# A two-layer trunk on one core: the planner's durations of TensorE's products are set to other numbers

## The chip, the cores and the metric

The kernel runs on one core of a Trainium2 chip. The metric is the device time of one execution in microseconds (us), lower is better. Profile times count from the start of the profiled execution's span.

## The reference

A trunk of two layers works on 256 latent tokens and 256 context tokens of width 1024. In each layer the modulated input goes through one wide projection, then through three mixers side by side (a bidirectional gated linear attention, GLA, in chunks of 64; a latent attention, MLA, with low-rank queries and keys; a convolution module), and the merged result through an output projection. Then comes a gated FFN with a convolution of width 3. A LayerNorm closes both halves. In the last layer the context only feeds the latent stream.

```python
def _trunk_layer(x, xc, mod, cmod, p, cos, sin, last):
    shift1, scale1, gate1, shift2, scale2, gate2 = [m[:, None, :] for m in jnp.split(mod, 6, axis=-1)]
    ...
    y, yc = _token_mixer(x * (1 + scale1) + shift1, xc * (1 + cscale1) + cshift1, p, cos, sin, last)
    x = _layer_norm(DN_ALPHA * x + gate1 * y, p['ln1_g'], p['ln1_b'])
    x = _layer_norm(DN_ALPHA * x + gate2 * _conv_ffn(x * (1 + scale2) + shift2, p), p['ln2_g'], p['ln2_b'])
    ...

def _conv_ffn(h, p):
    u = _depthwise_conv(h @ p['ffn_wup'], p['ffn_dw'], p['ffn_db'])
    g, v = jnp.split(u, 2, axis=-1)
    return (jax.nn.silu(g) * v) @ p['ffn_wdown']
```

## The kernel before

All values are float32. A large product is made of three products of rounded parts (`mm3`): a weight tile comes raw by a DMA on SyncE's queue (`wr`, four buffers), ScalarE casts its rounded high part (`wh`, three buffers), VectorE subtracts it for the low part (`wl`, three buffers), and TensorE adds up wh·xh, wh·xl and wl·xh. The inputs (`xm`, and `gy`, `my`, `cy`, `hd` further on) are split in the same way. Such products are of type F32R and have 256 or 512 columns; the products of the GLA units, of the norms (`sq` and `macc` times a constant) and of the attention are plain F32.

VectorE also has work that isn't wanted soon: `jk`, the rows of the modulation (w_ada) for later norms, `cv`, the taps of the two convolutions, and `gt`, the gates of the merge. Between mixer and FFN stands a norm: VectorE forms the sums (`macc`), takes off the mean (`xa`), ScalarE squares (`sq`), VectorE adds up the squares; TensorE adds over partitions (`pm_1473` in layer 0), VectorE picks from it (`dg`, a reduction to `sm`), GpSimd takes the power (`sm_1484`), TensorE spreads it (`pm_1485`), VectorE scales `xa`, ScalarE modulates it to `xm` and casts.

No instruction is issued where the program's code calls it. Class `Order` stands in for the engines' interface: `add` records each instruction with its dependences, `cost` gives it a duration, and `plan` is a list scheduler that starts instructions on five in-order engines (`ENGS`) when inputs and buffers are free, the one with the least latest start first. `back` finds the latest starts from the end of a plan, and `best` goes through eight such rounds and keeps the order whose planned end is the smallest. `emit` (line 294) then issues everything in that order, so that every row of the trace has line L294, and rows are told apart by the names of their tiles. A tile's number is counted up by the program; a row of an order names it, a row of the trace doesn't.

The durations of `cost` thus decide the order in which each engine takes its instructions, for all engines, and nothing else.

## Time and profile before

| | |
|---|---|
| three runs | 1907.19, 1908.35, 1911.92 us |
| median | 1908.35 us |
| span of the profiled execution | 1908.6 us |
| TensorE busy | 1854.9 us, 97% |
| VectorE busy | 1616.0 us, 85% |
| ScalarE busy | 1001.4 us, 52% |
| DMA | 312 MB, 164 GB/s on average |

Busy TensorE time in the profile is the union of matmuls that overlap; a row's own duration is therefore longer than the distance from its start to the next one's. Where a rate is read, it is the count of rows by the time of a stretch that is full. Names: PE is TensorE, PEld its weight loads, DVE VectorE, ACT ScalarE, POOL GpSimd, SP SyncE.

### The profile page before, as it was taken

The page shows a single profiled execution, that of the slowest core. Times are in us where ns is not written, and L with a number is a line of the kernel's source. Part 1 is how long each engine was busy: PE and PEld are TensorE (multiplying, and loading weights), DVE is VectorE, ACT ScalarE, POOL GpSimd, SP SyncE. Part 2 cuts the span into 40 slices and gives each one's busy share as a digit, 9 for nine tenths or more (in the row PEclk, how much of TensorE's full clock was granted, in tenths as well). Part 3 has the DMA queues.
Part 4 walks back from the last instruction along what each step waited for, and adds up shares of the span by engine and source line. Part 5 has one row for each costly group of instructions (what it writes and reads, how often), then busy time and mean ns, then how long its engine had stood idle before and what let it go on. Part 6 is the DMA issues. An engine that isn't in the chain of part 4 may idle for free.

```text
span 1908.6 us, 30907 instructions
## 1 busy us (share of the span) xinstructions
PE 1854.9 (97%) x11868; PEld 1661.8 (87%) x11868; DVE 1616.0 (85%) x2801; ACT 1001.4 (52%) x1564; POOL 21.1 (1%) x22
## 2 busy tenths in 40 slices
PE   6999999999999999989999999999899999989997
PEld 2889998887888888968888999999899889989997
DVE  2799999999899985899999766797978998878865
ACT  1863454246666264564443445864444675667643
POOL 0000000000000000000000000000000000000000
PEclk9999999999999999989999999999999999999999
DMA  7533247733223586566555667623265327846563
GB/s 269 178 113 104 89 138 236 250 112 120 84 90 114 160 257 201 171 205 210 186 188 176 194 178 213 190 67 105 63 189 172 99 95 245 263 155 210 181 181 93
DMA packets 116628, 312.18 MB, mean 164 GB/s; under 512 B 13376, under 2 KB 39232, under 8 KB 116480
## 3 DMA queue, kind: packets, MB, share of 16 engines
q1 hardware_dynamic: 116480, 310.21, 51.2%
q8 instruction: 93, 1.52, 0.3%
q14 instruction: 55, 0.45, 0.1%
HBM read 284.73 MB, written 25.43 MB: 163 GB/s over the span
## 4 chain that ended last, share of the span: by engine, by line
PE 53%; DVE 2%; ACT 1%; issue 0%; POOL 0%; ACTq 0%; DVEq 0%; POOLq 0%
PE pm L294 53%; DVE e L294 1%; ACT wh L294 0%; ACT xa L294 0%; DVE att L294 0%; DVE xa L294 0%; ACT xm L294 0%; DVE wl L294 0%; POOL sm L294 0%; DVE kd L294 0%; DVE sm L294 0%; DVE dg L294 0%; DVE cv L294 0%; DVE qe L294 0%; ACT kc L294 0%
## 5 line engine op out<-in xcount | busy, mean ns | idle before, releaser
L294 PE MATMUL pm<-xm,wh 128*128 128x256 f32 (+1 forms) x3536 | 872.6, 338 | 14.4 <-ACT xm L294 9.8
L294 ACT CAST wh<-wr 128x1024 fp32r<-128x1024 f32 (+2 forms) x394 | 401.8, 1021 | 599.7 <-PE pm L294 479.4
L294 PEld LDWEIGHTS pm<-xm,wh 128*128 128x128 f32 x3536 | 607.5, 191 | 84.1 <-ACT xm L294 11.2
L294 PE MATMUL pm<-xm,wl 128*128 128x256 f32 (+1 forms) x1768 | 591.3, 336 | 0.2 <-DVE wl L294 0.2
L294 DVE TENSOR_TENSOR wl<-wr,wh 128x1024 fp32r<-128x1024 f32 (+1 forms) x398 | 471.3, 1186 | 138.9 <-ACT wh L294 132.2
L294 PEld LDWEIGHTS pm<-xm,wl 128*128 128x128 f32 x1768 | 337.0, 191 | 37.7 <-issue 4.0
L294 DVE SCALAR_TENSOR_TENSOR cv<-h,vec,cv 128x512 f32<-128x512 f32 (+1 forms) x480 | 276.8, 611 | 1.1
L294 DVE SCALAR_TENSOR_TENSOR jk<-wr,crep 128x1024 f32<-128x1024 f32 x160 | 194.6, 1216 | 2.5 <-DMA wr<-in_w_adt_dram 2.4
L294 PE MATMUL pm<-hd,wh 128*128 128x256 f32 x1056 | 191.0, 283 | 0.0
L294 PEld LDWEIGHTS pm<-hd,wh 128*128 128x128 f32 x1056 | 165.0, 192 | 0.2
L294 PE MATMUL pm<-hd,wl 128*128 128x256 f32 x528 | 149.4, 283 | 0.0
L294 DVE SCALAR_TENSOR_TENSOR u<-pm,vec,u 128x255 f32<-128x255 f32 (+1 forms) x180 | 106.2, 601 | 1.8 <-ACT u L294 1.0
L294 PEld LDWEIGHTS pm<-hd,wl 128*128 128x128 f32 x528 | 101.3, 192 | 0.0
L294 PE MATMUL pm<-wh,xm 128*128 128x256 f32 x512 | 93.7, 283 | 0.0
L294 PEld LDWEIGHTS pm<-wh,xm 128*128 128x128 f32 x512 | 80.4, 192 | 0.4 <-issue 0.2
L294 PE MATMUL pm<-wl,xm 128*128 128x256 f32 x256 | 72.9, 285 | 0.0
L294 PE MATMUL pm<-ay,wh 128*128 128x256 f32 x384 | 69.7, 284 | 0.0
L294 ACT ACT_TABLE_LOAD x50 | 64.2, 1283 | 5.6 <-DMA ct<-in_cT_dram 2.4
L294 ACT ACTIVATE u<-pm,vec 128x256 f32<-128x256 f32 (+1 forms) x90 | 59.0, 660 | 12.9 <-PE pm L294 12.9
L294 PE MATMUL pm<-gy,wh 128*128 128x512 f32 (+1 forms) x256 | 62.5, 336 | 0.0
L294 PE MATMUL pm<-cy,wh 128*128 128x512 f32 (+1 forms) x256 | 62.5, 336 | 0.0
L294 PE MATMUL pm<-my,wh 128*128 128x512 f32 (+1 forms) x256 | 62.3, 336 | 0.0
(190 smaller groups left out, 2668.9 us busy)
## 6 DMA issues: line engine op xcount, KB each, us to landing
wr<-in_w_in_dram SPq DMA_DIRECT2D x124, 512.0 KB, 4.2
wr<-in_w_up_dram SPq DMA_DIRECT2D x90, 512.0 KB, 4.3
wr<-in_w_adt_dram SPq DMA_DIRECT2D x80, 512.0 KB, 3.7
wr<-in_w_sq_dram SPq DMA_DIRECT2D x72, 512.0 KB, 4.2
wr<-in_w_down_dram SPq DMA_DIRECT2D x48, 512.0 KB, 3.8
wr<-in_w_down_dram SPq DMA_DIRECT2D x24, 384.0 KB, 3.1
wr<-in_w_ada_dram SPq DMA_DIRECT2D x16, 512.0 KB, 4.4
wr<-in_w_v_dram SPq DMA_DIRECT2D x16, 512.0 KB, 3.8
```

What stands on the lines that cost most here:

```text
L294: method(*args, **kw)
```

## The change

In `Order.cost` the durations of two kinds of TensorE products change. One of F32R operands with n columns was n/2400 + 0.003 us, and is n/2400 + 0.0133 us (512 columns: 0.2163 to 0.2266; 256: 0.1097 to 0.1200). One of plain F32 was four times (n/2400 + 0.003), at least 0.42 us below 32 columns; it is 4n/2400 + 0.005, at least 0.222 (128 columns: 0.2253 to 0.2220; 1 column: 0.42 to 0.222). The set of instructions stays, but for the loads of ScalarE's function tables, which follow from the order: 52 where there were 50.

```diff
             if ins[0].dtype == F32R:
-                return n / 2400 + 0.003
+                return n / 2400 + 0.0133
             w = ins[0].shape[-1]
             if w <= 32:
                 return n / 2400 * 1.15 + 0.01
-            return max(4 * (n / 2400 + 0.003), 0.42 if n < 32 else 0.0)
+            return max(4 * n / 2400 + 0.005, 0.222)
```

What that does to the order is seen below, in three places; the rows stand in the order of the engine's list.

TensorE at the norm between mixer and FFN of layer 0, before: `pm_1506` and `pm_1514` are the first two tiles of the FFN's up-projection for one stream, `pm_1473` the norm's sum of squares for the other.

```order
L294 MATMUL pm_1506<-xm_1357,wh_1504 128x256
L294 MATMUL pm_1472<-macc_1471,cst 128x256
L294 MATMUL pm_1506<-xm_1357,wh_1504 128x256
L294 MATMUL pm_1514<-xm_1357,wh_1512 128x256 x2
L294 MATMUL pm_1473<-sq_1481,cst 128x256
L294 MATMUL pm_1506<-xm_1357,wl_1505 128x256
L294 MATMUL pm_1506<-xm_1358,wh_1504 128x256 x2
L294 MATMUL pm_1506<-xm_1358,wl_1505 128x256
```

The same place now, from the last product of `pm_1506` on:

```order
L294 MATMUL pm_1506<-xm_1364,wl_1505 128x256
L294 MATMUL pm_1514<-xm_1357,wl_1513 128x256
L294 MATMUL pm_1514<-xm_1358,wh_1512 128x256 x2
L294 MATMUL pm_1514<-xm_1358,wl_1513 128x256
L294 MATMUL pm_1514<-xm_1359,wh_1512 128x256 x2
L294 MATMUL pm_1514<-xm_1359,wl_1513 128x256
L294 MATMUL pm_1514<-xm_1360,wh_1512 128x256 x2
L294 MATMUL pm_1473<-sq_1481,cst 128x256
```

`pm_1473` stood behind 2 products of each tile; now the other 22 of `pm_1506` and 9 of `pm_1514` are ahead of it.

VectorE at the same place, before: `sq` are the sums of squares, `wl` the low parts of up-projection weights, `dg` and `sm` the norm's chain.

```order
L294 TENSOR_TENSOR xa_1463<-xa_1463,pm_1472 128x256
L294 TENSOR_TENSOR sq_1480<-sq_1479,sq_1480 128x256
L294 SCALAR_TENSOR_TENSOR jk_1466,mod_163<-wr_1464,crep 128x1024
L294 TENSOR_TENSOR sq_1481<-sq_1480,sq_1481 128x256
L294 TENSOR_TENSOR wl_1505<-wr_1503,wh_1504 128x1024
L294 TENSOR_TENSOR dg_1482<-pm_1473,cst 128x256
L294 SCALAR_TENSOR_TENSOR jk_1509,mod_163<-wr_1508,crep 128x1024
L294 TENSOR_REDUCE sm_1483<-dg_1482 128x2
L294 TENSOR_TENSOR xm_1364<-xm_1431,xm_1364 128x256
L294 TENSOR_SCALAR sm_1483<-sm_1483 128x2
L294 SCALAR_TENSOR_TENSOR jk_1510,mod_163<-wr_1508,crep 128x1024
L294 TENSOR_TENSOR wl_1513<-wr_1511,wh_1512 128x1024
```

And now:

```order
L294 TENSOR_TENSOR sq_1479<-sq_1478,sq_1479 128x256
L294 TENSOR_TENSOR wl_1521<-wr_1519,wh_1520 128x1024
L294 TENSOR_TENSOR sq_1480<-sq_1479,sq_1480 128x256
L294 SCALAR_TENSOR_TENSOR mod_163<-mod_163,vec_95 128x8
L294 TENSOR_TENSOR sq_1481<-sq_1480,sq_1481 128x256
L294 SCALAR_TENSOR_TENSOR jk_1509,mod_163<-wr_1508,crep 128x1024
L294 TENSOR_TENSOR dg_1482<-pm_1473,cst 128x256
L294 TENSOR_TENSOR wl_1526<-wr_1524,wh_1525 128x1024
L294 TENSOR_REDUCE sm_1483<-dg_1482 128x2
L294 SCALAR_TENSOR_TENSOR jk_1510,mod_163<-wr_1508,crep 128x1024
L294 TENSOR_SCALAR sm_1483<-sm_1483 128x2
L294 TENSOR_TENSOR wl_1535<-wr_1533,wh_1534 128x1024
```

`jk_1466` has gone ahead of the sums; `wl_1505` and `wl_1513` stand ahead of `sq_1478` and `sq_1479`, `wl_1521` between `sq_1479` and `sq_1480`; `wl_1526` and `wl_1535` have come into the chain behind `dg_1482`, and `jk_1517` follows on `wl_1535`.

VectorE in the first GLA unit of layer 1, before: `v` takes the values out of PSUM, `att` masks the scores, `e` and `kd` are decayed keys and queries.

```order
L294 TENSOR_TENSOR v_2216<-pm_2218,vb_2112 128x512
L294 TENSOR_TENSOR wl_2287<-wr_2285,wh_2286 128x1024
L294 COPY_PREDICATED att_2224<-lmask,pm_2227 128x512
L294 TENSOR_TENSOR wl_2291<-wr_2289,wh_2290 128x1024
L294 TENSOR_TENSOR e_2236<-cum_2219 128x128x2
L294 COPY_PREDICATED att_2224<-lmask,pm_2229 128x512
L294 TENSOR_TENSOR e_2236<-cum_2219 128x128x2 x2
L294 COPY_PREDICATED att_2224<-lmask,pm_2231 128x512
L294 TENSOR_TENSOR e_2236<-cum_2219 128x128x2
L294 TENSOR_TENSOR kd_2241<-kd_2241,pm_2240 128x512
L294 TENSOR_TENSOR kd_2245<-kd_2245,pm_2244 128x512 x2
L294 TENSOR_TENSOR e_2238<-cum_2219 128x256
```

And now:

```order
L294 TENSOR_TENSOR wl_2287<-wr_2285,wh_2286 128x1024
L294 TENSOR_TENSOR v_2216<-pm_2218,vb_2112 128x512
L294 TENSOR_TENSOR wl_2291<-wr_2289,wh_2290 128x1024
L294 COPY_PREDICATED att_2224<-lmask,pm_2227 128x512
L294 TENSOR_TENSOR e_2236<-cum_2219 128x128x2
L294 COPY_PREDICATED att_2224<-lmask,pm_2229 128x512
L294 TENSOR_TENSOR e_2236<-cum_2219 128x128x2 x2
L294 COPY_PREDICATED att_2224<-lmask,pm_2231 128x512
L294 TENSOR_TENSOR e_2236<-cum_2219 128x128x2
L294 COPY_PREDICATED att_2224<-lmask,pm_2233 128x512
L294 TENSOR_TENSOR e_2238<-cum_2219 128x256
L294 COPY_PREDICATED att_2224<-lmask,pm_2235 128x512
```

`wl_2287` and `v_2216` have changed places, and the copies of `pm_2233` and `pm_2235` have come ahead of the `kd` rows; the products e × kq and the four `kd` rows follow.

VectorE in the output projection of the GLA of layer 0, before (`wl_696` is row 409 of its list):

```order
L294 TENSOR_TENSOR wl_687<-wr_685,wh_686 128x1024
L294 SCALAR_TENSOR_TENSOR jk_674,mod_96<-wr_673,crep 128x1024
L294 SCALAR_TENSOR_TENSOR cv_285<-h_280,vec_94,cv_285 128x512
L294 SCALAR_TENSOR_TENSOR jk_675,mod_96<-wr_673,crep 128x1024
L294 SCALAR_TENSOR_TENSOR cv_274<-h_269,vec_94,cv_274 128x512
L294 TENSOR_TENSOR wl_696<-wr_694,wh_695 128x1024
```

And now (`wl_696` is row 420):

```order
L294 TENSOR_TENSOR wl_687<-wr_685,wh_686 128x1024
L294 SCALAR_TENSOR_TENSOR jk_675,mod_96<-wr_673,crep 128x1024
L294 TENSOR_TENSOR gt_648<-pm_658,gt_648 128x512
L294 SCALAR_TENSOR_TENSOR jk_683,mod_96<-wr_682,crep 128x1024
L294 TENSOR_TENSOR gt_660<-pm_667,gt_660 128x512
L294 SCALAR_TENSOR_TENSOR jk_684,mod_96<-wr_682,crep 128x1024
L294 TENSOR_TENSOR wl_696<-wr_694,wh_695 128x1024
```

Gates and modulation rows that stood behind `wl_696` are ahead of it; TensorE takes its tile at the same place as before.

## Rows read from the trace of the kernel before

**Rows 1.** The page: span, busy time of each engine with its share of the span and instructions, and from the costliest groups the loads of ScalarE's tables.

```profile
span 1908.6 us, 30907 instructions
PE 1854.9 (97%) x11868; PEld 1661.8 (87%) x11868; DVE 1616.0 (85%) x2801; ACT 1001.4 (52%) x1564; POOL 21.1 (1%) x22
...
L294 ACT ACT_TABLE_LOAD x50 | 64.2, 1283 | 5.6 <-DMA ct<-in_cT_dram 2.4
```

**Rows 2.** Busy time by stretch in two stretches of one kind of product each, 512 columns in the first and 256 in the second: the stretch and its length, then PE, PEld, DVE, ACT, POOL busy with counts, the granted clock of TensorE, the DMA engines' share and GB/s.

```profile
912.00:960.00 48.00, 48.00 (x213) 39.78 (x212) 46.75 (x70) 21.25 (x29) 0.00 (x0) 1.00 0.57 184
1824.00:1872.00 48.00, 48.00 (x403) 48.00 (x402) 27.84 (x37) 19.94 (x26) 0.00 (x0) 1.00 0.63 182
```

**Rows 3.** Busy time by stretch, with the columns of rows 2, for stretches in which TensorE isn't full and for 96 to 384 us.

```profile
0.00:48.00 48.00, 31.42 (x117) 11.91 (x117) 13.84 (x41) 7.05 (x12) 0.20 (x4) 0.93 0.79 269
...
96.00:336.00 240.00, 240.00 (x1451) 213.02 (x1450) 234.75 (x384) 117.15 (x145) 5.20 (x4) 1.00 0.43 138
336.00:384.00 48.00, 48.00 (x214) 39.74 (x213) 45.76 (x72) 10.48 (x11) 0.00 (x0) 1.00 0.78 248
...
792.00:840.00 48.00, 38.52 (x266) 35.54 (x265) 44.55 (x96) 33.16 (x69) 3.23 (x2) 0.89 0.53 174
...
1248.00:1296.00 48.00, 46.87 (x382) 45.89 (x382) 47.05 (x89) 27.84 (x41) 0.00 (x0) 1.00 0.20 65
...
1344.00:1392.00 48.00, 42.31 (x324) 40.88 (x323) 45.96 (x93) 18.27 (x28) 0.00 (x0) 0.96 0.15 45
...
1440.00:1488.00 48.00, 46.26 (x379) 45.47 (x378) 45.08 (x91) 23.11 (x37) 2.65 (x2) 1.00 0.60 187
...
1680.00:1728.00 48.00, 41.35 (x304) 39.42 (x304) 36.94 (x76) 32.67 (x65) 0.70 (x1) 0.93 0.51 166
...
1872.00:1908.00 36.00, 26.12 (x199) 25.01 (x197) 19.02 (x42) 12.15 (x23) 0.69 (x1) 0.90 0.22 69
```

**Rows 4.** Timelines at the norm between mixer and FFN of layer 0, engine by engine (VectorE, TensorE, GpSimd, ScalarE): start, duration, engine, line, operation, tiles, count, and in brackets the idle time before and what ended it.

```profile
813.25 0.75 DVE L294 TENSOR_TENSOR xa<-xa,pm 128x256 f32<-128x256 f32 x2
...
818.24 0.42 DVE L294 TENSOR_TENSOR sq<-sq,sq 128x256 f32<-128x256 f32 x1
818.58 1.22 DVE L294 SCALAR_TENSOR_TENSOR jk<-wr,crep 128x1024 f32<-128x1024 f32 x1
...
819.72 0.42 DVE L294 TENSOR_TENSOR sq<-sq,sq 128x256 f32<-128x256 f32 x1
820.06 1.22 DVE L294 TENSOR_TENSOR wl<-wr,wh 128x1024 fp32r<-128x1024 f32 x1
...
826.71 0.87 DVE L294 SCALAR_TENSOR_TENSOR xa<-xa,vec,pm 128x256 f32<-128x256 f32 x2 [0.68 <-PE pm L294]
...
820.20 1.22 PE L294 MATMUL pm<-sq,cst 128*128 128x256 f32 x2 [5.83 <-DVE sq L294]
...
822.14 0.41 PE L294 MATMUL pm<-xm,wl 128*128 128x256 f32 x1
...
824.06 0.41 PE L294 MATMUL pm<-xm,wl 128*128 128x256 f32 x1
...
829.99 0.50 PE L294 MATMUL pm<-xm,wh 128*128 128x256 f32 x2 [0.69 <-ACT xm L294]
831.25 0.50 PE L294 MATMUL pm<-xm,wh 128*128 128x512 f32 x1 [0.75 <-ACT wh L294]
...
823.93 1.51 POOL L294 TENSOR_TENSOR sm<-sm,mhalf 128x2 f32<-128x2 f32 x1 [22.23 <-DVE sm L294]
...
828.57 1.08 ACT L294 ACTIVATE xm<-xa,mod 128x256 f32<-128x256 f32 x2
```

**Rows 5.** Busy time by stretch around the same norm, with the columns of rows 2.

```profile
815.00:820.00 5.00, 0.00 (x0) 0.00 (x0) 5.00 (x14) 2.41 (x7) 0.00 (x0) 0.57 0.00 0
820.00:826.00 6.00, 5.80 (x24) 5.18 (x25) 5.82 (x11) 1.04 (x1) 1.51 (x1) 0.51 0.60 182
826.00:830.00 4.00, 3.31 (x29) 3.10 (x28) 3.32 (x6) 3.73 (x8) 0.00 (x0) 1.00 0.77 257
```

**Rows 6.** The first GLA unit of layer 1: timelines of VectorE and TensorE, and between them TensorE's waits in 1270 to 1284 us (who waited for whom, us in total, times, longest).

```profile
1270.62 0.69 DVE L294 TENSOR_TENSOR v<-pm,vb 128x512 f32<-128x512 f32 x1 [0.95 <-PE pm L294]
1271.23 1.22 DVE L294 TENSOR_TENSOR wl<-wr,wh 128x1024 fp32r<-128x1024 f32 x1
...
1282.08 0.71 DVE L294 COPY_PREDICATED att<-lmask,pm 128x512 f32<-128x512 uint8 x1
...
PE pm L294 <- DVE e L294: 1.1, 2, 0.9
...
1283.20 1.03 PE L294 MATMUL pm<-v,kd 128*128 128x256 f32 x4
```

**Rows 7.** TensorE's waits in the second GLA unit of layer 1, 1357 to 1383 us, with the same columns.

```profile
PE pm L294 <- DVE e L294: 5.1, 4, 3.2
```

**Rows 8.** Timelines of VectorE and TensorE at the norm of the MLA's keys in layer 1.

```profile
1480.34 1.22 DVE L294 TENSOR_TENSOR wl<-wr,wh 128x1024 fp32r<-128x1024 f32 x1
...
1484.60 1.16 PE L294 MATMUL pm<-cst,sm 128*128 128x128 f32 x8 [1.74 <-POOL sm L294]
```

**Rows 9.** Timelines of VectorE at `wl_696` and of TensorE at its first use.

```profile
356.42 1.23 DVE L294 TENSOR_TENSOR wl<-wr,wh 128x1024 fp32r<-128x1024 f32 x1
...
366.69 0.39 PE L294 MATMUL pm<-gy,wl 128*128 128x512 f32 x1
```

## Prediction

> **What bounds the kernel now.** I read the page's busy shares first, then the busy time by stretch, then the timelines around the stretches where TensorE is not full. TensorE is busy for 97% of the span, VectorE for 85%, ScalarE for 52% [rows 1]. In the stretch of 48 us that is nothing but 512-column products, 213 of them take 48.0 us, 0.225 us each; in one of 256-column products 403 take 48.0 us, 0.119 us each [rows 2]. The old numbers of the plan were 0.2163 and 0.1097, the new ones are 0.2266 and 0.1200: the new plan is told the truth, the old one was told a TensorE that is 4 to 8% too fast. But the instructions are the same, so wherever TensorE has been full it stays at the same rate, and the change can only move its idle time. The table by stretch shows how little of that there is [rows 3]: 16.6 us before 48 us, 9.5 in 792 to 840, 1.1 in 1248 to 1296, 5.7 in 1344 to 1392, 1.7 in 1440 to 1488, 6.7 in 1680 to 1728, 9.9 at the end. In the remaining stretches it is full, and there only a new wait could show. VectorE is nearly full beside it from 96 to 384 us (234.75 of 240, then 45.76 of 48).
>
> The order of the instructions is practically the same in the first 50 us and from 1680 us on, so the idle time there (33 us in the three places) stays: 0. That leaves four places.
>
> **1. The norm between mixer and FFN of layer 0, 810 to 834 us.** Before, VectorE sums the squares, ends the last sum (sq_1481) at 820.06 and only then makes wl_1505, the low part that the first FFN tile wants; TensorE waits 5.83 us, takes the sum's product pm_1473 at 820.20, and works at that tile while the norm's chain runs [rows 4]. Now VectorE makes wl_1505, wl_1513 and wl_1521 between the sums, and TensorE takes 31 products of the two tiles ahead of pm_1473.
>
> Start of the filling: from 813.25, where the sums' inputs begin, 12 short rows of VectorE (0.34 us from start to start, 818.24 to 818.58) give 817.3; wl_1505 follows and takes 1.14 (as a jk row of as many columns, 818.58 to 819.72). TensorE resumes at 818.4 and not at 820.2. The last sum: 817.3 + 3 × 1.14 + 4 × 0.34 + 0.1 = 822.2, so 2.1 later than before.
>
> Products ahead of pm_1473: the granted clock falls to half in this wait (0.57 in 815 to 820, 0.51 in 820 to 826, 1.00 from 826 on) [rows 5], and then nine products took 1.92 us (822.14 to 824.06), 0.213 each. Before, the half clock lasted 5.7 us after work was resumed; so 27 products at 0.213 and 4 at 0.119 take 6.2, and pm_1473 starts at 824.6 where it started at 820.2: +4.4. With a full clock it would be 822.1 (+1.9), with a half one throughout 825.0 (+4.8).
>
> From pm_1473 to GpSimd: before 3.73 us (820.20 to 823.93). Now: product 0.65 at a full clock, dg 0.34, wl_1526 1.14, the reduction 0.34, jk_1510 1.14, sm 0.3 = 3.9: GpSimd starts at 828.5. To xa: GpSimd 1.51 and the product pm_1485 with its hand-overs 0.74, so 830.75; wl_1535 and jk_1517 are put between sm and xa on VectorE, 2.3 us, and end at 830.7, hidden behind GpSimd. Before, xa started at 826.71: +4.1. From xa to the first product of the next tiles 3.28 us before (826.71 to 829.99), 3.2 now as no weight cast lies between on ScalarE: 834.0, +4.0.
>
> All the work in front of that product is the same set in both (both FFN tiles are complete), so the 4.0 is lost. Given back: before, 14 products, 2.1 us of work, took from 829.99 to 833.30, with 0.75 of waiting for wh_1534; now the casts and low parts are ready: -0.8 (0 to -1.2). And a second fall of the clock: the two tiles end at 824.6 + 0.5 + 15 × 0.119 = 827, then TensorE is idle for 7 us but for pm_1485, longer than the 5.83 us after which rows 5 show half clock. A half clock for 5.7 us costs 2.85 us of work where TensorE is the limit; right after the norm ScalarE is, with three rows like xm's 0.54 us (1.08 for two), 1.6, per feature tile against 1.4 of TensorE at full clock (six products of 0.119, three of 0.225), so I take half of it: +1.4 (0 to +2.85). Sum: 4.0 - 0.8 + 1.4 = **+4.6**. Bounds: with the clock full all the time 4.0 - 2.5 - 1.2 = +0.3; with all against it 4.0 + 0.4 + 2.85 = +7.2.
>
> [...]
>
> **2. The first GLA unit of layer 1, 1270 to 1283 us.** Before, TensorE waits twice, 1.1 us in all, for the products e × kq [rows 6], and VectorE had waited 0.95 for v's product. Now wl_2287 (1.14) is made in that wait, and one att copy (0.71) comes in: VectorE's chain behind v, which ran without a break from 1271.23 to 1282.08, where the last e × kq ended, has the same rows otherwise and is 1.14 - 0.71 = 0.4 shorter; it now ends on the last kd row at 1281.7, and the state products that started at 1283.20 can start at 1281.8. TensorE has 1.1 to give: I take **-1.3** (-1.1, the two waits, to -1.4, the whole shift).
>
> **3. The second GLA unit and the key norm of layer 1.** The second unit's four waits are 5.1 us, the longest 3.2 [rows 7]. Its chain on VectorE, from cum to the last e × kq, has the same rows in both orders and ends the wait, so the idle time stays; TensorE gets a little more done ahead of it, so it is not paid for behind: **+0.5** (-1.5 to +1.5, a row of 1.14 and one of 0.34 more or less on the chain). At 1484.60 TensorE waits 1.74 us for GpSimd; between dg and the reduction stands a low part of 1024 columns (1.14), now one of 384 columns (by its share 0.45) [rows 8]: -0.7; but low parts that the next tiles want come later there: **-0.5** (-0.7 to +2).
>
> **4. Layer 0's low parts, 96 to 385 us, where both engines are full.** Background rows of VectorE (jk, cv, gt) are moved ahead of the low parts of weights. The worst is wl_696: it ended at 357.6 and was first used at 366.69, 9.0 us of cover [rows 9]. It is now eleven rows further back in VectorE's list; at 0.71 (an att copy) to 1.14 us a row that is 8 to 12.5 us, so the cover may be short by up to 3.5. VectorE's own idle time in the stretch (2.24 of 48) takes up most of it, and what is done early is not done later. **+0.5** (0 to +3). Elsewhere in these stretches the covers stay positive. Two more table loads on ScalarE (52 where there were 50) are hidden by its 48% of idle time: 0, and 2.6 at 1.28 each [rows 1] if not.
>
> **Sum.** 4.6 - 1.3 + 0.5 - 0.5 + 0.5 = +3.8 on the profiled 1908.6 us, which stands 0.25 above the median of the three runs: 1912.4, so 1912 us, 0.2% slower. By the bounds alone: -3 to +12, or +15 with the table loads. What a measurement can tell from no change is about 0.3%, 5.7 us.
>
> **Rivals.**
> *It is faster.* The waits of the two GLA units of layer 1 go, since the plan now gives the plain F32 products there other times: 1.1 + 5.1, and 1.9 for the half clock behind the longest wait (a granted 0.96 over 1344 to 1392, so 0.04 × 48) [rows 3]. With the layer-0 norm at +0.3: 1908.6 - 8.1 + 0.3 = 1901. For it: in place 2 the order does just this. Against it: in the second unit the chain is as long as before. It decides from where the norm costs less than 2 us and the second unit gains 4. Chance 0.2.
> *It comes out even.* The norm's second cold spell doesn't come, pm_1473 isn't held up by the half clock, and the gain of the first unit pays for it: 0.3 - 1.3 + 0.5 = 1908. Inside the same bound as the forecast. Chance 0.15.
> *It is clearly slower.* The norm costs its upper bound, 7, by the two cold spells, and the low parts of layer 0 come late at several places at once (3), as VectorE is full beside TensorE from 96 us on: 1908.6 + 10 - 1.3 = 1917. For it: the clock in rows 5 and eleven rows at wl_696. Against: the idle time of VectorE. Chance 0.35.
>
> **How the numbers follow.** The forecast has 0.3, with the even case 0.45, faster 0.2, slower 0.35. The likeliest lies at 1912, with 1908 to 1914 for it alone; 8 in 10 reach from the faster rival's 1901 to beyond the slower one's 1917, its other unknowns (2 at the key norm, 2.6 of table loads) added: 1901 to 1921.
>
> **What the profile will show.** Right: a TensorE that resumes near 818 us, pm_1473 near 824, the first product after the norm near 834, a granted clock under 1 in 834 to 840; 0 instead of 1.1 us idle near 1280; the waits near 1370 to 1380 as before. Wrong if idle time of TensorE shows between 100 and 400 us in amounts above 3 us, if the longest wait near 1378 is gone, or if the norm costs nothing since the early products are taken at a full clock.

## The result and the profile after

The changed kernel takes 1930.53 us (median of four runs, 1927.73 to 1932.15), the kernel before 1909.21 us (four runs, 1907.19 to 1911.92). The ratio is 1.0106, with a 95% interval of 1.0093 to 1.0120: slower by 21 us. The forecast was 1912, its range ended at 1921.

The page of the changed kernel, in the lines of [rows 1]:

```profile
span 1930.4 us, 30899 instructions
PE 1866.2 (97%) x11868; PEld 1669.2 (86%) x11868; DVE 1613.6 (84%) x2801; ACT 1003.7 (52%) x1566; POOL 25.8 (1%) x22
...
L294 ACT ACT_TABLE_LOAD x52 | 66.7, 1283 | 5.7 <-DVE e L294 2.5
```

The same products, VectorE 2.4 us less busy, and one number that stands out: GpSimd is busy for 25.8 us, not 21.1, with the same 22 instructions. The busy time by stretch, with the columns of [rows 3], moved along where the work lies later:

```profile
0.00:48.00 48.00, 31.27 (x117) 11.95 (x117) 13.87 (x41) 7.08 (x12) 0.20 (x4) 0.92 0.78 270
96.00:336.00 240.00, 236.27 (x1426) 209.18 (x1425) 233.30 (x386) 113.81 (x143) 9.38 (x4) 0.99 0.39 127
336.00:384.00 48.00, 48.00 (x214) 39.75 (x213) 43.15 (x75) 10.08 (x10) 0.00 (x0) 1.00 0.85 278
804.00:852.00 48.00, 34.98 (x235) 32.74 (x234) 44.75 (x95) 30.44 (x64) 3.05 (x2) 0.82 0.54 180
1260.00:1308.00 48.00, 47.42 (x386) 46.53 (x385) 47.85 (x89) 34.07 (x47) 0.00 (x0) 1.00 0.21 67
1364.00:1412.00 48.00, 41.05 (x298) 39.53 (x297) 45.36 (x92) 17.58 (x25) 0.00 (x0) 0.89 0.09 28
```

Where TensorE never waited in 240 us [rows 3], it now waits 3.7 us, and its clock is below 1.00 there (0.99); GpSimd's four powers in that stretch take 9.38 us, not 5.20. Idle time above 3 us between 100 and 400 us was one of the prediction's own signs of being wrong.

To place the loss I gave each product the distance from start to start that its kind has at the full clock (F32R of 256 and 512 columns 0.120 and 0.227 us, plain F32 of 128 columns 0.223, two rows of the trace at 0.112, and so on), and took what the next one starts later than that as lost. The work so counted is 1812.9 us in both kernels; lost are 81.8 us before and 103.5 after, by places of the program (in brackets the prediction's numbers of its places):

| place | before | after | difference | predicted |
|---|---|---|---|---|
| 125 us, norm of the first GLA unit, layer 0 | 0.0 | 6.6 | +6.6 | in place 4: no loss |
| norm between mixer and FFN, layer 0 (1) | 14.0 | 18.3 | +4.3 | +4.6 |
| second GLA unit, layer 1 (3) | 8.3 | 11.3 | +3.0 | +0.5 |
| merge and start of layer 1, 1211 to 1253 us | 0.3 | 2.9 | +2.6 | not seen |
| first GLA unit, layer 1 (2) | 1.9 | 2.4 | +0.5 | -1.3 |
| key norm, layer 1 (3) | 3.6 | 2.1 | -1.5 | -0.5 |
| half-clock spell near 47 us, 3.4 us long before, 6.8 after | 4.0 | 5.3 | +1.3 | 0 |
| nine others, 0.3 to 1.0 each | | | +5 | +0.5 |

### The profile page after: what moved, and what is told of

It reads as the page before. It is cut to its first block, busy times and chain, and to the rows that moved or that the text cites. A ratio compares the mean times of both kernels' runs of the same rounds, so it can differ in the third digit from the quotient of the medians.

```text
span 1930.4 us, 30899 instructions
## 1 busy us (share of the span) xinstructions
PE 1866.2 (97%) x11868; PEld 1669.2 (86%) x11868; DVE 1613.6 (84%) x2801; ACT 1003.7 (52%) x1566; POOL 25.8 (1%) x22
## 4 chain that ended last, share of the span: by engine, by line
PE 49%; DVE 5%; ACT 2%; issue 1%; POOL 0%; ACTq 0%; DVEq 0%; POOLq 0%
PE pm L294 49%; DVE cv L294 2%; DVE wl L294 1%; DVE e L294 1%; ACT wh L294 1%; ACT xm L294 0%; ACT xa L294 0%; DVE xa L294 0%; POOL sm L294 0%; DVE sm L294 0%; DVE att L294 0%; DVE dg L294 0%; DVE st L294 0%; DVE sq L294 0%; DVE fs L294 0%
```

## The experiments

**The block at 125 us.** In the changed kernel, GpSimd's power, TensorE's products around it, and VectorE's rows:

```profile
124.52 5.15 POOL L294 TENSOR_TENSOR sm<-sm,mhalf 128x4 f32<-128x4 f32 x1 [124.08 <-DVE sm L294]
...
125.85 0.39 PE L294 MATMUL pm<-xm,wh 128*128 128x512 f32 x1
129.72 1.65 PE L294 MATMUL pm<-cst,sm 128*128 128x128 f32 x6 [3.48 <-POOL sm L294]
...
123.94 0.41 DVE L294 TENSOR_TENSOR e<-cum 128x256 f32<-128x256 f32 x1
124.28 0.16 DVE L294 TENSOR_SCALAR sm<-sm 128x4 f32<-128x4 f32 x1
124.34 4.45 DVE L294 TENSOR_TENSOR e<-cum 128x256 f32<-128x256 f32 x13
...
129.50:136.00 6.50, 6.28 (x19) 5.32 (x20) 2.62 (x6) 3.67 (x4) 0.16 (x1) 0.51 0.08 13
```

The last column but two of the stretch is the granted clock: behind the wait of 3.48 us it is at half (0.51 in these 6.5 us). The power of 128x4 takes 5.15 us: it begins 0.18 us behind the start of 13 short rows of VectorE (`e` from `cum`, both in SBUF) and ends 0.88 us behind their end at 128.79. The same power and VectorE's rows around it before:

```profile
122.67 1.01 POOL L294 TENSOR_TENSOR sm<-sm,mhalf 128x4 f32<-128x4 f32 x1 [122.23 <-DVE sm L294]
...
122.10 0.41 DVE L294 TENSOR_TENSOR e<-cum 128x256 f32<-128x256 f32 x1
...
122.50 0.74 DVE L294 SCALAR_TENSOR_TENSOR h<-pm,vec,sg 128x512 f32<-128x512 f32 x1
123.16 1.21 DVE L294 SCALAR_TENSOR_TENSOR jk<-wr,crep 128x1024 f32<-128x1024 f32 x1
```

There it took 1.01 us, and an `h` row, with an operand in PSUM (TensorE's result memory), stood behind `sm`, the small row that releases GpSimd. The theory: the run of rows with both operands in SBUF keeps GpSimd out. The rival: something else holds it. In `e1_h_behind_sm` the changed order has one row moved, `h_269` from ahead of `dg_258` to behind `sm_259` (`eps` is that small row; a pair asks that the first stand ahead of the second; in the code a tile has another number than in the orders, `sm163` is `sm_259`):

```diff
+        eps = f("DVE", "sm163")[-1]
+        return [(eps, h)]
```

> The changed kernel with one row of VectorE moved six places back: the gate row h (its one matrix operand from SBUF, the other from PSUM, 0.74 us) stands behind the norm's last small row sm instead of ahead of dg, so that GpSimd's power falls beside it and not beside the run of 13 e rows that read both operands from SBUF. Theory (GpSimd cannot get at its data while VectorE runs rows with two SBUF operands back to back): the power takes 1.0 us as in the kernel before instead of 5.15, TensorE's wait of 3.48 us at 126 us is gone, the half clock of 129.0 to 135.9 us too, and the time falls by 5.5 to 6.6 us, from 1930.4 to about 1924. Rival (the chain in front of GpSimd is late, or this power is slow by itself): the power still takes about 5 us, TensorE still waits 3 us, the time stays within 1 us of 1930.

Measured: 1925.85 us (1924.5 to 1928.14), ratio to before 1.0080 (1.0063 to 1.0097). GpSimd and VectorE there (the last line is cut off where the view ends; it is the same run of 13 rows):

```profile
123.29 1.01 POOL L296 TENSOR_TENSOR sm<-sm,mhalf 128x4 f32<-128x4 f32 x1 [122.85 <-DVE sm L296]
188.31 2.58 POOL L296 TENSOR_TENSOR sm<-sm,mhalf 128x4 f32<-128x4 f32 x1 [64.01 <-DVE sm L296]
...
122.71 0.42 DVE L296 TENSOR_TENSOR e<-cum 128x256 f32<-128x256 f32 x1
123.04 0.16 DVE L296 TENSOR_SCALAR sm<-sm 128x4 f32<-128x4 f32 x1
123.11 0.75 DVE L296 SCALAR_TENSOR_TENSOR h<-pm,vec,sg 128x512 f32<-128x512 f32 x1
123.77 2.43 DVE L296 TENSOR_TENSOR e<-cum 128x256 f32<-128x256 f32 x7
```

One row removes the whole 6.6 us at this place; of that 4.7 reach the end by the medians, 5.8 when each kernel is set against the kernel before in its own series. Two places got worse: the next power, at 188 us, takes 2.58 where the changed kernel has 1.44 (+1.65 there), and a half-clock spell of 3.4 us appears at 1295.6.

Then kernels of their own, which compute none of the reference: a 128x4 power is released, and VectorE runs rows of one kind behind the release.

> The disputed cost by itself; nothing of the reference is computed. GpSimd's power of 128x4 values is started eight times, each beside another run of VectorE: nothing; 13 subtractions of 256 columns with both operands in SBUF; 13 with one operand in PSUM; 6 scale-and-add rows of 512 columns with both in SBUF; 4 subtractions of 1024 columns with both in SBUF; 13 rows with a single SBUF operand; the first run with its fifth row reading PSUM; nothing. Theory (a row with two SBUF operands shuts GpSimd out, and between two such rows it does not get in): about 0.7 to 1.0 us beside nothing and beside PSUM rows; about the length of the run, 13 x 0.34 + 0.9 = 5.3, beside the 256-column SBUF rows; about 2 to 2.5 with the fifth row from PSUM; and beside the 512 and 1024 column rows the run's length too (4 to 5 us) if the same holds for them, 1.4 to 1.9 if GpSimd gets in at a boundary, as the rows of the kernel before suggest. Rival (GpSimd is only slow now and then): all eight within 0.7 to 2 us.

Measured in `mb_port`: 1.01 without rows, 1.12 beside 13 rows of 256 columns with both operands in SBUF, 1.01 beside a PSUM operand, 1.44 and 1.91 beside rows of 512 and 1024 columns. No power was held for the length of a run. But all rows wrote one tile, and the short ones stood 0.46 us from start to start where the kernel's stand 0.34 apart. With places of their own for the results, `mb_port2`:

> The disputed cost by itself again, nothing of the reference is computed. In the first trial every row wrote the same tile, so that a row began only when the one before it had ended (0.46 us from start to start), and the power took 1.0 to 1.9 us beside all of them. Now each row writes a place of its own. Beside the power of 128x4: nothing; 13 rows like e (subtraction of a broadcast column, both operands in SBUF); 13 plain ones of 256 columns with both in SBUF; 13 with one operand in PSUM; 6 of cv's kind with 512 columns; 4 of wl's kind with 1024; 13 like e with the fifth from PSUM; 13 like e with the fifth of cv's kind. Theory (short rows that overlap, 0.34 us from start to start and 0.42 long, leave GpSimd no gap, and it waits for the end of the run): beside nothing and beside PSUM rows 1.0 us; beside e rows and plain rows about 13 x 0.34 + 0.9 = 5.3; beside cv and wl rows 1.3 to 2; with the fifth row from PSUM about 2.5. Rival (what held the power up at 125 us is not VectorE's run): all below 2 us again.

Measured: 5.14 us beside 13 rows with two SBUF operands, 5.32 beside four low parts of 1024 columns, 1.01 beside a PSUM operand; but 1.12 beside 13 rows with a broadcast second operand, as `e` has it. The hold is real, and its condition was not the operands alone. Two more cases bear on it. Beside 1024-column rows, with `cv`'s kind right ahead in both, the power took 1.91 in `mb_port`, where each row begins 0.03 us behind the end of the one before, and 5.32 here, where it begins 0.08 ahead of that end. And with the fifth of 13 rows of `cv`'s kind (scale and add, 512 columns, both matrix operands in SBUF) it took 2.12 and ended 0.87 behind the fourth row: a row of another kind let it in. `e10_block_before` puts such a run of `e` rows behind the release in the order of before:

```diff
+        run = f("DVE", "e229", "cum220") + f("DVE", "e231", "cum220") + f("DVE", "e233", "cum220") + f("DVE", "e227", "cum220")
+        late = f("DVE", "jk206") + f("DVE", "wl202") + f("DVE", "cv178") + f("DVE", "cv189")
+        return [(h, dg)] + [(i, j) for i in run for j in late]
```

> Before's order with one stretch near 122 us rearranged on VectorE: h_269 (its operand in PSUM) moved ahead of dg_258, and jk_302, wl_298 and cv_274 moved behind eleven short rows e<-cum with both operands in SBUF, so that 8 or 9 of these run back to back (0.34 us apart) while GpSimd has its power sm_260, until o_254, which needs that power. Theory: such a run of rows keeps GpSimd out, so sm_260 takes about 3 us or longer in place of 1.01 us, as it took 5.15 us in the changed kernel beside 13 rows. Rival: the 5.15 us there came from something else in that order, and sm_260 takes 1.0..1.2 us here. The whole time stays within 1908..1912 by either, since the cover at this place holds 3 us or not.

Measured: 1909.9 us in one run, and the theory as put there fell:

```profile
122.97 1.11 POOL L296 TENSOR_TENSOR sm<-sm,mhalf 128x4 f32<-128x4 f32 x1 [122.53 <-DVE sm L296]
...
120.61 0.74 DVE L296 SCALAR_TENSOR_TENSOR h<-pm,vec,sg 128x512 f32<-128x512 f32 x1
121.28 0.68 DVE L296 TENSOR_TENSOR dg<-pm,cst 128x512 f32<-128x512 f32 x1
...
122.79 3.44 DVE L296 TENSOR_TENSOR e<-cum 128x256 f32<-128x256 f32 x10
```

Ten rows in one run, and the power takes 1.11. So I gave one power after the other the very rows of both kernels, A those of the changed one and B those of `e10_block_before` (each pair: the width of a block, and which of an `e` tile's four rows):

```diff
+            A = [(16, 0), (32, 3), (16, 1), (16, 2), (8, 0), (16, 3), (8, 1), (8, 2), (4, 0), (8, 3), (4, 1), (4, 2), (2, 0)]
+            B = [(64, 2), (32, 0), (64, 3), (32, 1), (32, 2), (16, 0), (32, 3), (16, 1), (16, 2), (8, 0)]
```

> A kernel of its own, which computes none of the reference: GpSimd's 128x4 power is released, and behind it VectorE runs one of these rows of subtractions back to back, in the shapes and strides that the rows e<-cum have. a0..a3: the 13 rows that stood behind sm_259 in the changed kernel (blocks of 16, 32, 16, 16, 8, 16, 8, 8, 4, 8, 4, 4, 2), four times. b0..b3: the 10 rows of e10_block_before (blocks of 64, 32, 64, 32, 32, 16, 32, 16, 16, 8), four times. s64 to s2: 12 rows of one block width, twice with different halves. Theory A, the width of the block decides (the second operand is one value repeated over the block, so wide blocks read little): all a take 4.5..5.3 us, all b 1.0..1.2, and the s rows go from 1.0..1.2 at 64 to 5 at 2 with one step between. Theory B, the instant at which the power and a row meet decides: equal sequences give unequal times, a and b mixed between 1.0 and 5.3. Theory C, neither: all a take 1.0..1.2, and what held the power in the changed kernel lies outside VectorE's rows.

Measured: 1.11 us for all four a, 4.13 for all four b, and in each pair of s rows 1.11 and 4.80. Neither the width of a block nor chance: every second power was held, whatever its rows.

> A kernel of its own again, which computes none of the reference: powers of GpSimd with rows of VectorE behind their release, as in mb_rows, but each power's tiles now stand 512 bytes apart, so that an address in them has no part in a turn. In order: five times the 13 rows of the changed kernel; four times those 13 rows followed by a power with no rows behind it; twice those rows followed by two such powers; then 13, 18, 18, 13, 7, 7, 8 and 8 rows. mb_rows had 1.11 us and 4.13 or 4.80 us strictly in turn, whatever the rows. Theory A, turns among the powers that meet such rows: 1.11 and about 5.1 in turn among these, whether or not powers without rows stand between, and the held ones last as long as their rows (18 rows about 6.8, 7 rows about 3.1). Theory B, turns among all powers: with one power without rows between, all alike; with two between, in turn. Theory C, the tile's address: all five at the start alike.

Measured: with the tiles 512 bytes apart the turns stay in the first five, 1.11, 5.14, 1.11, 5.13, 1.11; with one or two powers without rows between, all that have rows are free (1.11). The held ones last as long as the rows (18 rows 6.82, 13 rows 5.13, 8 rows 3.46, 7 rows 3.12). Theories B and C fall; A half, since its turns should have gone on past powers without rows. What all free ones had in common was that VectorE had just waited, for the power before (0.90 or 1.12 us) or, ahead of the first, for a transfer (2.06). `mb_pause` separates that from the turn:

> A kernel of its own, which computes none of the reference. In mb_turn a power was free (1.11 us) whenever VectorE had waited for something just before, and held to the end of its rows (5.13) whenever VectorE's rows ran up to its release without a pause; that also is the order in which a power followed one that had been free. This parts the two. Twice over: a power with no rows (n); 13 rows, the release, 13 rows (a); n; the same; then three times 13 rows, one, two or three rows with one operand (0.4 us each by the nearest rows), the release, 13 rows; n; three times the same with one, two or three rows with an operand in PSUM (0.7 us each); at the end n and three times rows behind the release alone. Theory A, the pause: whatever the power before was, rows right ahead of the release hold it (all a without filler 5.1 us, behind n too), and from some length of filler on it takes 1.1. Theory B, the turn: every power behind n takes 1.1 us though rows run up to it, and those behind one that was free take 5.1.

GpSimd's rows: a power without rows, one with rows ahead and behind, then with one and two one-operand rows between; further on with one and two rows with a PSUM operand. Below them VectorE's rows in the cases with one and two fillers:

```profile
16.22 1.01 POOL L1578 TENSOR_TENSOR rs<-va,mhalf 128x4 f32<-128x4 f32 x1 [0.35 <-DVE va L1577]
21.94 5.14 POOL L1578 TENSOR_TENSOR rs<-va,mhalf 128x4 f32<-128x4 f32 x1 [4.71 <-DVE va L1577]
32.12 5.14 POOL L1578 TENSOR_TENSOR rs<-va,mhalf 128x4 f32<-128x4 f32 x1 [5.05 <-DVE va L1577]
42.78 1.11 POOL L1578 TENSOR_TENSOR rs<-va,mhalf 128x4 f32<-128x4 f32 x1 [5.51 <-DVE va L1577]
...
63.72 5.14 POOL L1578 TENSOR_TENSOR rs<-va,mhalf 128x4 f32<-128x4 f32 x1 [5.31 <-DVE va L1577]
74.89 1.11 POOL L1578 TENSOR_TENSOR rs<-va,mhalf 128x4 f32<-128x4 f32 x1 [6.04 <-DVE va L1577]
...
27.19 4.45 DVE L1535 TENSOR_TENSOR e<-x 128x256 f32<-128x256 f32 x13
31.55 0.42 DVE L1574 TENSOR_SCALAR g<-x 128x512 f32<-128x512 f32 x1
...
37.37 4.45 DVE L1535 TENSOR_TENSOR e<-x 128x256 f32<-128x256 f32 x13
41.73 0.89 DVE L1574 TENSOR_SCALAR g<-x 128x512 f32<-128x512 f32 x2
42.53 0.16 DVE L1577 TENSOR_SCALAR va<-col 128x4 f32<-128x4 f32 x1
42.60 4.44 DVE L1535 TENSOR_TENSOR e<-x 128x256 f32<-128x256 f32 x13
```

Theory A, the pause, in both passes: a power behind an unhindered one is held too (21.94). What fits these cases is the time between the end of the last row with two SBUF operands ahead of the release and the start of the first one behind it. With 0.31 us (one filler, 31.64 to 31.95) and 0.59 (one PSUM row) the power is held for the whole run, with 0.78 (41.82 to 42.60) and more it is free. The kernels fit: 0 in the changed one (`e` ends at 124.35, the next starts at 124.34), 2.1 in `e10_block_before`, 0.64 in e1 (123.13 to 123.77), and 0.65 before. It also says what the broadcast rows of `mb_port2` were: VectorE had waited just ahead of them (1.13 us). In e1 and before, most of that time lies behind the release, in `mb_pause` all of it ahead; whether the two count alike, no run tests.

On the operands the traces show this much: beside rows with a PSUM operand a power took 1.01 us, in `mb_port` and in `mb_port2`, where VectorE had waited 0.90 us just ahead; a run of such rows closed around the release was not tried. Every 128x4 power of the two kernels and of the `mb_` ones that took 1.3 us or more ended 0.86 to 0.88 us behind the end of one of VectorE's rows. For the changed kernel's power at 195 us (1.44) that is the first row behind the release, a `cv` row; for the one at 125 us and those of the `mb_` kernels that were held for a whole run it is the last of 4 to 18 rows. Why one row in some cases and a whole run in others, no run shows.

**The two lines of the change apart.** `e2_only_f32r` has only the first, `e3_only_f32` only the second.

> One part of the change alone: only the duration of F32R products is set to the new number, the plain F32 ones keep the old. Theory (the new F32R numbers, which hold for nearly all of TensorE's time, make the plan put the weights' low parts and their products ahead of the norm's chain): the norm of layer 0 still resumes near 843 in place of 830 of the kernel before, and the time is 1918 to 1932. Rival (an order is sensitive to any number, and each place comes out by chance): the places that lost do not follow either line; the time may lie anywhere from 1900 to 1935.

> The other part alone: only the duration of plain F32 products is new, the F32R ones keep the old. Theory (this line matters in the GLA units only, and there little): within 6 us of the kernel before, 1903 to 1915, with the layer-0 norm as in the kernel before and the second GLA unit of layer 1 with its longer half clock if that comes from this line. Rival (an order is sensitive to any number): anywhere from 1900 to 1935, and the two parts do not add up to the whole +21.8.

Measured: 1932.46 us (1929.3 to 1933.23; ratio 1.0114, 1.0098 to 1.0129) with the F32R line, 1912.48 (1910.59 to 1914.32; 1.0011, 1.0002 to 1.0020) with the other. The norm's loss (19.5 lost at that place) and that of the start of layer 1 (2.7) are in the F32R line. The first GLA unit's gain is there with the F32 line alone (0.27 lost, where before had 1.9). The second unit's loss comes with either (11.1 and 12.3, where before had 8.3). The block at 125 us comes with neither alone: its power takes 1.01 us in both.

**The norm of layer 0.** In the changed kernel TensorE, GpSimd and VectorE, and two stretches:

```profile
831.07 0.58 PE L294 MATMUL pm<-xm,wl 128*128 128x256 f32 x1 [4.15 <-DVE wl L294]
...
836.86 0.60 PE L294 MATMUL pm<-sq,cst 128*128 128x256 f32 x2
...
842.33 1.16 PE L294 MATMUL pm<-cst,sm 128*128 128x128 f32 x4 [3.33 <-POOL sm L294]
846.28 1.44 PE L294 MATMUL pm<-xm,wh 128*128 128x256 f32 x4 [2.79 <-ACT xm L294]
...
840.77 1.51 POOL L294 TENSOR_TENSOR sm<-sm,mhalf 128x2 f32<-128x2 f32 x1 [28.20 <-DVE sm L294]
...
843.53 2.83 DVE L294 SCALAR_TENSOR_TENSOR xa<-xa,vec,pm 128x256 f32<-128x256 f32 x7 [0.67 <-PE pm L294]
...
831.00:835.50 4.50, 4.43 (x20) 4.43 (x21) 3.80 (x8) 0.00 (x0) 0.00 (x0) 0.50 0.69 221
842.30:849.00 6.70, 3.88 (x15) 3.49 (x16) 5.94 (x15) 4.95 (x13) 0.00 (x0) 0.51 0.62 226
```

The wait of 5.83 us [rows 4] is now 4.15, 3.33 and 2.79, and the clock is at half in two spells, as predicted. Two kernels tried to take the loss back by putting the chain first, both on top of e1:

```
e5_norm_first: pm_1473 ahead of the last three inputs of pm_1506, pm_1485 ahead of the last six of pm_1514;
  VectorE: wl_1521 and wl_1526 behind sm_1483, wl_1535 behind xa_1436, jk behind all xa
e8_norm_and_act: pm_1473 ahead of the last two inputs of pm_1506, pm_1485 ahead of the last three of pm_1514;
  VectorE: jk_1509 and wl_1526 behind sm_1483; wl_1535 behind the first low part of xm, jk_1510 and jk_1517 behind the third; ScalarE: wh_1534 behind the first casts of xm
```

> The kernel with the h row moved, and at the norm of layer 0 the norm's chain put first: pm_1473 into the middle of the tile pm_1506 in place of behind 31 products, pm_1485 among the first products of pm_1514, and on VectorE wl_1521, wl_1526, wl_1535 and the four jk rows behind the step of the chain that they stood ahead of. The early low parts wl_1505 and wl_1513 stay. Theory (the place lost by the order of the chain, worked out as +4.6 and measured as +4.3): TensorE's idle and slow time at this place falls by 4 to 6 us and the total from 1925.9 to 1920 to 1922. Rival (the place is set by ScalarE's and VectorE's work as such, and by the half clock): less than 2 us.

> This is e1_h_behind_sm (1925.85 us) with the norm of layer 0 put in a looser row than e5 had: pm_1473 15 matmul rows earlier on TensorE (1.7 us by rate), the ones-product pm_1485 ahead of the last 9 rows of pm_1514; on VectorE dg_1482, the sum and the epsilon of the mean square stand together, with jk_1509 and wl_1526 behind them and jk_1510, jk_1517, wl_1535 behind the first low parts; on ScalarE the cast wh_1534 stands behind the casts of xm_1357 and xm_1358 (u_1515 stays where it was, ahead of xa). Theory: in the changed kernel the norm costs 4.3 us more because its chain stands behind work that the new plan put ahead of it, so the excess of this place falls from 18.3..18.8 us to 14..16 us and the whole to 1921..1923. Rival: what the place costs is set by u_1515, which waits for the end of pm_1514 ahead of xa on ScalarE, and by the half clock, so the place stays at 18 or above as in e5 (22.1) and the time at 1925..1928.

Measured: 1927.91 us (1927.19 to 1931.33; ratio 1.0091, 1.0076 to 1.0106) and 1926.22 (1924.54 to 1930.34; 1.0089, 1.0074 to 1.0105). The place lost 22.1 and 20.4 us, against 18.8 in e1. TensorE's waits in e8, 805 to 850 us:

```profile
PE pm L296 <- DVE wl L296: 4.3, 1, 4.3
PE pm L296 <- ACT wh L296: 3.4, 3, 2.1
PE pm L296 <- ACT xm L296: 2.7, 1, 2.7
PE pm L296 <- DVE xm L296: 2.0, 1, 2.0
PE pm L296 <- POOL sm L296: 0.2, 1, 0.2
```

TensorE's wait for GpSimd is gone (3.33 to 0.2), and the first product of the next tiles comes 18.8 us behind the first one of these tiles, where it came 21.0 behind in e1 and 17.8 before. The total didn't follow. `xa` waits on ScalarE behind `u_1515`, which needs the end of `pm_1514`; behind that product TensorE waits 0.75 us for `wh_1534` and, with the `jk` rows put off until then, 2.0 for a later `xm`. The rival held in both. That the new order costs 4.3 us here is measured; that the chain's place in the lists is the cause is not shown, since moving it ahead gave nothing back.

**The clock.** Idle 128x128 products ahead of those that wait, into PSUM that the next product overwrites, keep TensorE busy. The lists say how many stand ahead of the first product into a tile, in the code's numbers (`pm1433` is `pm_1473`, `pm1474` is `pm_1506`, `pm2359` to `pm2365` are in the second GLA unit):

```diff
# e6_warm_gla, on top of e1
+WARM = {'pm2361': 6, 'pm2363': 8, 'pm2365': 11}
# e7_before_warm, on the order of before
+WARM = {'pm32': 18, 'pm1474': 6, 'pm1433': 25, 'pm1490': 3, 'pm2363': 4, 'pm2365': 13, 'pm3166': 12, 'pm3199': 12}
# e9_f32_warm, on top of e3
+WARM = {'pm32': 18, 'pm1432': 6, 'pm1474': 0, 'pm1433': 0, 'pm2359': 4, 'pm2361': 7, 'pm2363': 8, 'pm2365': 11, 'pm3166': 12, 'pm3199': 12}
```

> The kernel with the h row moved, and in the second GLA unit of layer 1 idle products into the three waits of 1.7, 2.0 and 2.7 us: 6, 8 and 11 products of 128 columns of a constant (0.22 us each) into the PSUM tile that the waiting products then overwrite. No wait gets shorter by it. Theory (that place is 3 us worse than in the kernel before for the clock alone: half clock for 10.2 us in place of 3.4, the waits themselves end when they did): the half clock of 1391 to 1401 us is gone and the total falls by 2.5 to 4.5, from 1925.9 to about 1922. Rival (the longer chain makes the loss): no gain, or a loss of up to 1 us as the idle products push the others back.

> The kernel before, its order untouched, with the same idle products in its long waits: 18 at 20 us, 6 and 25 and 3 at the norm of layer 0, 4 and 13 in the second GLA unit of layer 1, 12 and 12 at the norm of layer 1. Theory (a wait that brings the half clock costs its own length and the slow work behind it): the half clocks at 24, 816, 1379 and 1696 us are gone, 6.8 + 10.2 + 3.4 + 6.8 = 27 us of which some 16 fell on work at half speed, so 5 to 9 us less: 1900 to 1905, faster than both kernels. Rival (behind a wait the other engines are the limit, and a full clock only waits for them): 1907 to 1911, the same.

> This is e3_only_f32 (the duration of full-precision products alone, 1912.5 us) with idle 128x128 products on TensorE ahead of the products that wait (18 ahead of pm32, 6 ahead of the first product of layer 0's norm chain pm1432, 4, 7, 8 and 11 in the second unit of layer 1's GLA, 12 and 12 near 1700 us). Theory: the second GLA unit lost 4 us to a half-clock spell of 10.2 us; kept warm it costs 8 us or less, and with what such products gave before's order (3.5 us in all) the time is 1903..1907, below both kernels and below e7 (1906.96). Rival: behind these waits the other engines are the limit, as they were in e7, the spell only fills time that is waited in any case, and the time is 1908..1912.

Measured: e6 1924.89 us (1921.95 to 1927.17; ratio 1.0074, 1.0055 to 1.0093): the spell in the second GLA unit is gone, and the place loses 1.6 and 5.5 of idle products where it lost 11.0; the whole is 1 us below e1, inside its interval. e7 1906.96 (1906.07 to 1908.39; 0.9980, 0.9971 to 0.9989), the fastest here and below both kernels. e9 1908.86 (1907.13 to 1910.24; 0.9992, 0.9983 to 1.0000), 3.6 below e3 but not below e7; its list has 6 products at the norm of layer 0, and the half clock of 10.2 us there stayed. In e7 the clock stays full at the four places, as in this stretch with the second GLA unit:

```profile
1370.00:1390.00 20.00, 19.25 (x142) 18.09 (x143) 19.99 (x39) 6.29 (x12) 0.00 (x0) 1.00 0.16 52
```

Four half-clock spells, 27.2 us in all, went. TensorE had been busy for 19.1 us of them and waiting for the rest, so the clock itself, at 0.50 in them, was worth at most half of that, 9.6 us by estimate; 3.5 came back. The idle products took 20.7 us, and what TensorE lost beside them fell from 81.8 to 57.4. VectorE is busy for 19.99 of the 20 us above, which fits a pace that other engines set behind the waits, so that a slow TensorE was partly hidden; no run tests that by itself.

## Why the prediction was wrong

For one term of five the steps and the price came out as forecast, and the largest loss lay where the prediction had looked only for late low parts.

- **"Elsewhere in these stretches the covers stay positive"** (place 4) is the step that failed. It followed the low parts (wl_696 now ends at 368.9 and is first used at 375.3: the cover held, as forecast), and took GpSimd's powers to last as long as before. At 125 us one lasted 5.15 us in place of 1.01; with the half clock behind it that cost 6.6 us, 6.1 above the term. Two more of these powers grew, at 440 us (1.85 to 2.72) and 1320 us (1.13 to 1.83), and TensorE's wait for them grew from 0.80 to 1.23 us and from none to 0.67. The changed order has the `h` row ahead of `dg_258` and no longer behind `sm_259`; the prediction didn't read that as a change of a duration.
- **Place 1** came out as forecast: +4.3 against +4.6. All work at this place lies 11.8 us later (w_out ends at 822.57, before at 810.74); less that, wl_1505's first product comes at 819.2 (forecast 818.4), pm_1473 at 825.0 (824.6), GpSimd at 828.9 (828.5), xa at 831.7 (830.75), the first product of the next tiles at 834.5 (834.0), and the second cold spell came. Its reason, that a later chain is lost time one for one, isn't confirmed: in e8 that product came 2.3 us sooner than in e1, and the place lost 1.6 more. Part of the match may be luck.
- **Place 3, the second GLA unit**, was mis-sized: +3.0 against +0.5. The chain was as long as forecast to within its bound: the waits are 6.4 us, where they were 5.1 [rows 7]. But TensorE, which before had `ls` products to do between the waits, now has done them ahead of the first, so the waits follow each other with 1.1 and 1.9 us of products between (1.68, 2.01, 2.68), and the clock is at half from 1395.4 for 10.2 us, before 3.4.

```profile
1392.11 1.13 PE L294 MATMUL pm<-e 128*128 128x128 f32 x8 [1.68 <-DVE e L294]
1395.25 1.93 PE L294 MATMUL pm<-e 128*128 128x128 f32 x8 [2.01 <-DVE e L294]
1399.87 3.76 PE L294 MATMUL pm<-e 128*128 128x128 f32 x16 [2.68 <-DVE e L294]
...
1396.00:1405.00 9.00, 6.32 (x30) 6.05 (x30) 8.23 (x15) 4.41 (x8) 0.00 (x0) 0.50 0.00 0
```

- **Place 2**: +0.5 against -1.3. One of the two waits remains (0.6 of 1.1 us, [rows 6]), and the power at 1320 us takes the gain.
- **The key norm** gave 1.5 against 0.5: GpSimd's wait fell from 1.74 [rows 8] to 0.2, and no low part came late.
- **Not seen**: 2.6 us at the start of layer 1, in waits for `macc` (0.5), `fs` (0.9) and `ab` (0.5); the spell of half clock near 47 us, twice as long (+1.3). That spell isn't shown to follow from the change: in e1, where TensorE's whole order is that of the changed kernel and VectorE's the same up to 116 us, it is 3.4 us as before. The table loads cost nothing that shows.
- **The base** mixes two measures: 1908.6 is a span, and a span is 1.75 us shorter than the time of its execution (1930.4 and 1932.15). That is small beside the miss of 18.

The rival "clearly slower" had the right side, with 1917 in place of 1930; its mechanisms didn't make the difference: the norm's two cold spells came, but the norm cost 4.3 and not 7, and between 96 and 420 us TensorE waits for no low part.

## What to carry to other kernels

When an order changes, look not only for which rows are late but for what stands beside each GpSimd instruction that somebody waits for: 0.64 us or more without two-operand SBUF rows around the release (an `h` row behind it, two fillers ahead of it) kept a power at 1.0 to 1.1 us here, one row with a PSUM operand ahead of it (0.59 us) didn't; a run of such rows 0.34 us apart, closed around the release, made the power last as long as the run (13 rows, 5.15 us). A planner with truer durations of one engine can still give a worse order (here by 21 us): this plan puts each such power at a fixed 0.96 us and has no term for the clock. Waits that are short one by one cost more when nothing is left to do between them: in the second GLA unit of layer 1, +3.0 us.

## What the runs showed of the hardware

A 128x4 power of GpSimd lasted 5.15 us in the changed kernel and 6.82 and 3.12 in `mb_turn`, beside 13, 18 and 7 rows of VectorE that follow each other 0.34 us apart with both operands in SBUF, and ended 0.9 us behind the last; a pause of 0.31 or 0.59 us in such rows at the release didn't help, one of 0.64 to 0.78 did. That doesn't cover all: at 188 us in e1 and at 195 us in the changed kernel VectorE has the same rows at the same distances (`jk`, `sm`, `cv`, `jk`, `wl`), and the power takes 2.58 in one and 1.44 in the other. In e1 it ends 0.87 us behind the second row behind the release (`jk`), in the other 0.87 behind the first (`cv`); what decides that is open. Of 27.2 us of half clock that were kept at full clock, with TensorE busy for 19.1 of them, 3.5 came back.
